# Bias rows stored with 32 repeats from the scalar engine's queue, and shifted bias tables read 32 partitions at a time

## The chip, the core and the metric

The kernel runs on one core of a Trainium2 chip. The metric is device time in microseconds (us), the median of repeated runs. The engines that matter here are the tensor engine (PE, matrix products), the vector engine (DVE), the scalar engine (ACT) and the sync engine (SP), whose queue issues nearly all transfers. All engines run beside each other, each one through its own list of instructions in order, and wait for one another by semaphores.

## What is computed

A decoder trunk for 256 tokens of width 2048: one retention layer, then one block-sparse attention layer. Each has a squared-ReLU MLP of width 8192 and a gated per-layer embedding behind it. With 256 tokens there is one attention block, so attention is plain causal attention with 16 heads of 128. What the change touches is the position bias that is added to its logits:

```python
def t5_bucket(dist):
    n = jnp.maximum(dist, 0)
    ...
    return jnp.where(n < max_exact, n, large)
...
dist_own = qpos[:, None] - (blk * BLK + jnp.arange(BLK))[None, :]
l_own = jnp.einsum('hqd,hkd->hqk', qc, k_own, ...) * scale
l_own = jnp.where(dist_own[None] >= 0, l_own + bias_t[:, t5_bucket(dist_own)], NEG_INF)
```

The bias of a head depends on the distance of query and key alone, so one row of 384 numbers for each head (distances 255 to 0, then masked places) holds everything. A table for 128 queries is this row, shifted by one place from query to query.

## The kernel before

**Weights.** The time goes into streaming some 500 MB of float32 weights through PE. Weights come in units of 128 x 1024 numbers. `load` fetches two units in one transfer of 1 MB, `raw`, on SP's queue into one of three buffers. `conv` splits a unit into a high part `wh` (a cast on ACT, L218) and a low part `wl` (a subtraction on DVE, L219), with four buffers for each. In the phases that the change touches a unit is then 8 pairs of matmuls: 512 columns with `wh` (L158) and 256 columns with `wl` (L159). `run` walks over the units. For unit i it issues the load for unit i + 6 and the conversion of unit i + 3, then the matmuls of unit i, then the small tasks that were booked for unit i with `at`. There is no scheduler: each engine gets its instructions in the order in which this loop writes them.

**Bias rows.** `bias_rows` is booked 30 units before the end of the first MLP's `mlp_dn` stream (tiles `dn`). It loads the 32 x 16 bias table and a constant 33 x 384 matrix, makes 16 rows of 384 numbers by one product (`rows`, L608, copied to `bv` by DVE, L610), and two units later writes each row many times over into the scratch tensor `bvec` in device memory (`store`, L613). The many copies are there so that `table` can read a shifted table with a plain access pattern: partition p starts at place 383 p + 127 behind the head's first number, that is at place 127 - p of copy p.

**Tables.** The attention is done in four groups of four heads. Ahead of each group `table` (L639) reads two tiles `T`, 128 partitions x 2 heads x 256 numbers. They are used some ten units later, in `logits`, where DVE adds them (L679).

**Transfers and their semaphores.** Every transfer signals one of eight semaphores, taken in turn in program order (DMAHW0 to DMAHW7 in the rows of the order below). A transfer whose predecessor on the same semaphore isn't known to have landed waits for it first. A `raw` load also waits for DVE, which must have read the buffer.

Of the kernel before, what the change touches and what calls it, by code (L numbers as in the profile page):

```python
# [10 lines left out]
F32 = mybir.dt.float32  # L11
# [6 lines left out]
P = 128  # L18
S = 256
# [5 lines left out]
AH, DH = 16, 128  # L25
GH = 4
# [7 lines left out]
LEAD = 4  # L34
LOOK = 3
WARM = 8
G_RET, G_MLP0, G_PLE0, G_KV, G_ATT, G_MLP1, G_PLE1, G_FIN = range(8)


# [34 lines left out]
class Core:  # L74
# [3 lines left out]
        self.units, self.tasks = [], {}  # L78
        self.raws, self.ready = {}, {}

# [1 line left out]
    def unit(self, src, j, mm):  # L82
        self.units.append((src, j, mm))
        return len(self.units) - 1
# [37 lines left out]
                fn()  # L122

    def steps(self, i, gen, each=1):
        """the steps of an evacuation: the first after unit i, then each of them per unit"""
        if not next(gen, True):
            self.at(i + 1, lambda: self.more(i + 1, gen, each))

# [15 lines left out]
    def small(self, name):  # L144
        return self.wp.tile([P, S], F32, name=name, tag="small", bufs=6)

# [1 line left out]
    def mm_a(self, ps, wh, wl, rhs, first, last, narrow=False):  # L148
        mm = self.nc.tensor.matmul
        for k in range(8):  # L150
# [8 lines left out]
            mm(ps[:, S:], wl[:, c], rhs[k][:, :S], start=False, stop=last and k == 7)  # L159

    def phase_a(self, name, src, base, tiles, per, lead, rhs, evac, narrow=(), rush=()):
        """tiles of [128 outputs, 256 tokens]; rhs(k) is the (H|L) tile of 128 inputs;
        a narrow tile is summed in one half of its bank"""
        banks, ends = {}, {}
        for j, (n, u) in enumerate(order_a(tiles, per, lead)):
            def mm(wh, wl, n=n, u=u):
                if u == 0:
                    banks[n] = self.bank(f"{name}{n}")
                self.mm_a(banks[n], wh, wl, [rhs(u * 8 + k) for k in range(8)], u == 0, u == per - 1, n in narrow)
            i = self.unit(src, base + j, mm)  # L170
            if u == per - 1:
                ends[n] = i
                self.at(i, lambda n=n, i=i: self.steps(i, evac(n, banks.pop(n)), 4 if n in rush else 2 if n == tiles - 1 else 1))
        return ends

    def phase_d(self, name, src, rhs, evac):
        """4 tiles of [128 outputs, 256 tokens] by units of 4 tiles of inputs and 2 of outputs"""
        banks = {}
        for u in range(4):
            for v in range(2):  # L180
                def mm(wh, wl, u=u, v=v):
                    m = self.nc.tensor.matmul
                    for n in (2 * v, 2 * v + 1):
                        if u == 0:
                            banks[n] = self.bank(f"{name}{n}")
                        ps = banks[n]
                        for j in range(4):
                            c, x = slice((4 * (n % 2) + j) * P, (4 * (n % 2) + j + 1) * P), rhs(4 * u + j)
                            m(ps, wh[:, c], x, start=u + j == 0, stop=False)
                            m(ps[:, S:], wl[:, c], x[:, :S], start=False, stop=u == 3 and j == 3)  # L190
                i = self.unit(src, 2 * u + v, mm)
                if u == 3:
                    for n in (2 * v, 2 * v + 1):
                        self.at(i, lambda n=n, i=i: self.steps(i, evac(n, banks.pop(n))))

    def phase_b(self, name, src, base, rhs, evac):
        """[256 tokens, 512 outputs] as two banks"""
        banks = []
        for u in range(KD // 2):
            def mm(wh, wl, u=u):  # L200
                if u == 0:
                    banks.extend(self.bank(f"{name}{t}") for t in range(2))
                for j in range(2):
                    k = 2 * u + j
                    x, c = rhs(k), slice(j * 512, (j + 1) * 512)
                    for t in range(2):
                        a, b = slice(t * P, (t + 1) * P), slice(S + t * P, S + (t + 1) * P)
                        mm_ = self.nc.tensor.matmul
                        mm_(banks[t], x[:, a], wh[:, c], start=k == 0, stop=False)  # L209
                        mm_(banks[t], x[:, a], wl[:, c], start=False, stop=False)  # L210
                        mm_(banks[t], x[:, b], wh[:, c], start=False, stop=k == KD - 1)  # L211
            i = self.unit(src, base + u, mm)
        self.at(i, lambda: evac(banks))
        return i

# [1 line left out]
    def split(self, dst_h, dst_l, src):  # L217
        self.nc.scalar.copy(dst_h, src)  # L218
        self.nc.vector.tensor_sub(dst_l, src, dst_h.bitcast(F32))  # L219

    def fold(self, dst, ps):
        """dst = the two halves of a bank added"""
        self.nc.scalar.copy(dst, ps[:, :S])  # L223
        self.nc.vector.tensor_add(dst, dst, ps[:, S:])  # L224

    def scaled_h(self, n, g):
        """(h * g) of tile n: the high part of H|L"""
        t = self.slot(f"x{g}_{n}", dt=F32R)
        gs = self.g[:, g, n:n + 1]
        self.nc.scalar.activation(t[:, :S], self.h[n], AF.Copy, scale=gs)  # L230
        return t
# [16 lines left out]
            self.nc.vector.tensor_add(self.acc, self.acc, sq)  # L248

    def rsqrt(self, dst, src, eps, n):  # L250
        """dst = (src + eps) ** -0.5; small tiles"""
        v = self.nc.vector
        a = self.cp.tile([P, n], F32, name="rs_a", tag="rs_a", bufs=2)
        y = self.cp.tile([P, n], F32, name="rs_y", tag="rs_y", bufs=2)
        w = self.cp.tile([P, n], F32, name="rs_w", tag="rs_w", bufs=2)
        v.tensor_scalar_add(a, src, eps)
        v.tensor_single_scalar(y.bitcast(I32), a.bitcast(I32), 1, ALU.logical_shift_right)
        v.tensor_scalar(y.bitcast(I32), y.bitcast(I32), -1, 0x5F3759DF, op0=ALU.mult, op1=ALU.add)
        for c in (3.0, 12.0, 768.0):
            v.tensor_mul(w, y, y)  # L260
            v.tensor_mul(w, w, a)
            v.scalar_tensor_tensor(y, w, c, y, op0=ALU.subtract, op1=ALU.mult)
        v.tensor_scalar_mul(dst, y, -1.0 / 8192.0)
# [22 lines left out]
        self.at(i, self.stats_a)  # L286
        self.at(i + 2, lambda: self.stats_b(**kw))

# [1 line left out]
    def start(self):  # L290
        nc, cp, io = self.nc, self.cp, self.io
        self.ones = cp.tile([P, 2], F32, name="ones")
# [2 lines left out]
        nc.scalar.activation(warm, self.ones, AF.Silu)  # L295
        self.warm(WARM)
        self.hh = [cp.tile([P, 4, S], F32, name=f"h{q}") for q in range(4)]
# [191 lines left out]
        return hi, lo  # L489

    def finish(self, n, gains):
        """tile n of the stream is whole: its scaled splits and its squares"""
        xs = [self.scaled_h(n, g) for g in gains]
        sq = self.square(n)
        yield
        for x, g in zip(xs, gains):
            self.scaled_l(n, g, x)
        self.gather(n, sq)
        self.xx[n] = xs[0]
        if len(xs) > 1:  # L500
            self.x2[n] = xs[1]
# [93 lines left out]
    def bias_rows(self, i):  # L595
        nc, cp, io = self.nc, self.cp, self.io
        st = {}

        def load():
            st["rb"] = cp.tile([33, AH], F32, name="relb")  # L600
            nc.vector.memset(st["rb"][32:33], NEG)
            nc.sync.dma_start(st["rb"][:32], io["rel_bias"])
            st["oh"] = self.slot("oh", (33, 384))
            nc.sync.dma_start(st["oh"], io["onehot"])

        def rows():
            ps = self.aux("bv")
            nc.tensor.matmul(ps[:AH, :384], st["rb"], st["oh"], start=True, stop=True)  # L608
            st["bv"] = self.slot("bv", (AH, 384))
            nc.vector.tensor_copy(st["bv"], ps[:AH, :384])  # L610

        def store():
            nc.sync.dma_start(io["bvec"], st["bv"][:, None, :].to_broadcast([AH, P, 384]))  # L613
        self.at(i, load)
        self.at(i + 6, rows)
        self.at(i + 8, store)

    def attention(self):
        nc = self.nc
        mm = nc.tensor.matmul  # L620
        first = len(self.units)
# [8 lines left out]
        for g in range(AH // GH):  # L630
            b, st = len(self.units), {}

            def table(st=st, g=g):
                st["T"] = []
                bv = self.io["bvec"]
                for j in range(0, GH, 2):
                    t = self.slot("T", (P, 2, S))
                    src = bass.AP(tensor=bv.tensor, offset=bv.offset + (g * GH + j) * P * 384 + 127, ap=[[383, P], [P * 384, 2], [1, S]])
                    nc.sync.dma_start(t, src)  # L639
                    st["T"] += [t[:, 0], t[:, 1]]  # L640
            self.at(b, table)

# [92 lines left out]
def program(nc, io):  # L735
    with tile.TileContext(nc) as tc, tc.manual_schedule(), \
# [1 line left out]
            tc.tile_pool(name="slots", bufs=59) as sp, \  # L738
            tc.tile_pool(name="psum", bufs=1, space=bass.MemoryType.PSUM) as pp, \
            tc.tile_pool(name="dram", bufs=1, space=bass.MemoryType.DRAM) as dp:  # L740
        io["bvec"] = dp.tile([AH, P, 384], F32, name="bvec")
        c = Core(nc, tc, (cp, wp, sp, pp), io)
        c.at(-1, c.start)
        c.retention()
# [71 lines left out]
```

## Time and profile before

| | |
|---|---|
| time, median of 3 runs | 2832.81 us (2832.39 to 2833.46) |
| span of the profiled execution | 2831.3 us |
| PE busy | 2798.1 us, 99% |
| DVE busy | 1807.1 us, 64% |
| ACT busy | 1347.6 us, 48% |
| moved by DMA | 521.95 MB, mean 184 GB/s |

The span runs from the first to the last instruction. The median is 1.5 us longer: that lies around the span, in starting and ending. PE is busy nearly all the time, so what counts is where PE is not, and where it is busy at less than its usual pace. The views used are the list of waits (who waited for whom), the windows (busy time and PE's granted clock in a stretch), the timeline of one engine, the chain of work that ended last, and the transfers with their time from issue to landing.

### The profile page before, as it was taken

What the parts mean: (1) busy time and instruction counts of PE and PEld (TensorE: products, weight loads), DVE (VectorE), ACT (ScalarE), POOL (GpSimd) and SP (SyncE); (2) the same over time, 40 slices, a digit from 0 to 9 for tenths busy, and PEclk for the clock granted to TensorE, in tenths of its full rate; (3) what the DMA queues carried; (4) which work ended last, traced back from release to release, by engine and by line L of the source; (5) the groups of instructions that cost most, each with busy time, mean ns of one, the idle gap of its engine ahead of it and who ended that gap; (6) DMA issues with size and microseconds to landing.
All of it is one profiled execution on the core that took longest, in us unless ns stands there. A gap on an engine that the chain in (4) does not pass through costs nothing.

```text
span 2831.3 us, 37950 instructions
## 1 busy us (share of the span) xinstructions
PE 2798.1 (99%) x15482; PEld 2417.3 (85%) x15482; DVE 1807.1 (64%) x2633; ACT 1347.6 (48%) x1901; POOL 0.2 (0%) x4
## 2 busy tenths in 40 slices
PE   9999999999999999999979999999999999999998
PEld 7888888888888888888868888888888888888887
DVE  7766666655566555665647876667665556666566
ACT  5444444444454434444436655555444434444454
POOL 0000000000000000000000000000000000000000
PEclk9999999999999999999989999999999999999998
DMA  6455555555555555555574554545555555555553
GB/s 233 179 181 181 181 182 182 182 199 186 178 194 182 190 184 189 183 189 181 191 185 179 198 181 176 180 170 185 187 184 188 183 189 186 187 190 182 194 182 119
DMA packets 78667, 521.95 MB, mean 184 GB/s; under 512 B 8443, under 2 KB 14492, under 8 KB 16796
## 3 DMA queue, kind: packets, MB, share of 16 engines
q1 hardware_dynamic: 78492, 519.52, 52.1%
q8 instruction: 121, 1.98, 0.3%
q14 instruction: 54, 0.44, 0.0%
HBM read 514.25 MB, written 5.24 MB: 183 GB/s over the span
## 4 chain that ended last, share of the span: by engine, by line
PE 98%; DMA 1%; DVE 0%; ACT 0%; SPq 0%; issue 0%; DVEq 0%; ACTq 0%
PE up L158 17%; PE dn L158 17%; PE up L159 9%; PE dn L159 8%; PE ret_out L158 4%; PE gt L158 4%; PE qk L158 4%; PE ret_out L159 2%; PE ak L158 2%; PE att_o L158 2%; PE aq L158 2%; PE v L209 2%; PE v L211 2%; PE v L210 2%; PE g L209 2%; PE g L211 2%
## 5 line engine op out<-in xcount | busy, mean ns | idle before, releaser
L219 DVE TENSOR_TENSOR wl<-raw,wh 128x1024 fp32r<-128x1024 f32 (+1 forms) x970 | 1180.9, 1221 | 643.9 <-ACT wh L218 633.0
L218 ACT CAST wh<-raw 128x1024 fp32r<-128x1024 f32 (+1 forms) x970 | 1014.6, 1049 | 774.2 <-PE dn L158 277.8
L158 PE MATMUL dn<-a,wh 128*128 128x512 f32 x2048 | 725.2, 399 | 14.5 <-ACT wh L218 14.5
L158 PE MATMUL up<-x,wh 128*128 128x512 f32 x2048 | 724.1, 399 | 0.0
L159 PE MATMUL dn<-a,wl 128*128 128x256 f32 x2048 | 576.1, 281 | 0.5 <-DVE wl L219 0.5
L159 PE MATMUL up<-x,wl 128*128 128x256 f32 x2048 | 575.1, 281 | 0.0
L158 PEld LDWEIGHTS dn<-a,wh 128*128 128x128 f32 x2048 | 385.7, 188 | 111.0 <-ACT wh L218 14.8
L158 PEld LDWEIGHTS up<-x,wh 128*128 128x128 f32 x2048 | 384.8, 188 | 95.8
L159 PEld LDWEIGHTS dn<-a,wl 128*128 128x128 f32 x2048 | 387.9, 189 | 1.0 <-DVE wl L219 1.0
L159 PEld LDWEIGHTS up<-x,wl 128*128 128x128 f32 x2048 | 387.0, 189 | 0.0
L158 PE MATMUL ret_out<-ot,wh 128*128 128x512 f32 x512 | 181.1, 399 | 0.0
L158 PE MATMUL gt<-x,wh 128*128 128x512 f32 x480 | 170.0, 399 | 0.0
L158 PE MATMUL qk<-x,wh 128*128 128x512 f32 x448 | 159.1, 399 | 0.0
L223 ACT COPY t<-up 128x256 f32<-128x256 f32 x128 | 47.6, 372 | 231.7 <-PE up L159 231.7
L159 PE MATMUL ret_out<-ot,wl 128*128 128x256 f32 x512 | 143.8, 281 | 0.0
L159 PE MATMUL gt<-x,wl 128*128 128x256 f32 x480 | 134.7, 281 | 0.0
L224 DVE TENSOR_TENSOR t<-t,up 128x256 f32<-128x256 f32 x128 | 53.9, 421 | 119.9 <-ACT t L223 119.8
L159 PE MATMUL qk<-x,wl 128*128 128x256 f32 x448 | 125.8, 281 | 0.0
L158 PEld LDWEIGHTS ret_out<-ot,wh 128*128 128x128 f32 x512 | 96.2, 188 | 24.0
L158 PEld LDWEIGHTS gt<-x,wh 128*128 128x128 f32 x480 | 90.2, 188 | 22.1
L158 PEld LDWEIGHTS qk<-x,wh 128*128 128x128 f32 x448 | 84.2, 188 | 20.3
L209 PE MATMUL v<-wh,x 128*128 128x512 f32 x256 | 100.5, 392 | 0.0
(311 smaller groups left out, 3459.3 us busy)
## 6 DMA issues: line engine op xcount, KB each, us to landing
raw<-mlp_up SPq DMA_DIRECT2D x128, 1024.0 KB, 4.9
raw<-mlp_dn SPq DMA_DIRECT2D x128, 1024.0 KB, 4.9
raw<-ret_in SPq DMA_DIRECT2D x94, 1024.0 KB, 4.9
raw<-att SPq DMA_DIRECT2D x48, 1024.0 KB, 4.9
raw<-ret_out SPq DMA_DIRECT2D x32, 1024.0 KB, 4.9
raw<-ple_gate SPq DMA_DIRECT2D x32, 1024.0 KB, 4.9
raw<-att_o SPq DMA_DIRECT2D x16, 1024.0 KB, 4.9
raw<-ple_up SPq DMA_DIRECT2D x4, 1024.0 KB, 4.9
```

Source lines behind the costliest of these rows:

```text
L158: mm(ps, wh[:, c], rhs[k], start=first and k == 0, stop=False)
L159: mm(ps[:, S:], wl[:, c], rhs[k][:, :S], start=False, stop=last and k == 7)
L209: mm_(banks[t], x[:, a], wh[:, c], start=k == 0, stop=False)
L210: mm_(banks[t], x[:, a], wl[:, c], start=False, stop=False)
L211: mm_(banks[t], x[:, b], wh[:, c], start=False, stop=k == KD - 1)
L218: self.nc.scalar.copy(dst_h, src)
L219: self.nc.vector.tensor_sub(dst_l, src, dst_h.bitcast(F32))
L223: self.nc.scalar.copy(dst, ps[:, :S])
L224: self.nc.vector.tensor_add(dst, dst, ps[:, S:])
```

## The change

`store` writes 32 copies of each row, not 128: 16 x 32 x 384 numbers (768 KB) and not 16 x 128 x 384 (3072 KB). It is issued from ACT's queue and not from SP's. `table` can then no longer read 128 partitions in one pattern, since there are only 32 copies. It reads four times 32 partitions, with a start that is q places earlier for partitions q to q + 31. What lands in `T` is the same. 8 transfers of 256 KB become 32 transfers of 64 KB, all on SP's queue. The scratch tensor shrinks accordingly. (The diff also drops some comments, which shifts no instruction.)

```diff
+BR = 32
...
         def store():
-            nc.sync.dma_start(io["bvec"], st["bv"][:, None, :].to_broadcast([AH, P, 384]))
+            nc.scalar.dma_start(io["bvec"], st["bv"][:, None, :].to_broadcast([AH, BR, 384]))
...
                 for j in range(0, GH, 2):
                     t = self.slot("T", (P, 2, S))
-                    src = bass.AP(tensor=bv.tensor, offset=bv.offset + (g * GH + j) * P * 384 + 127, ap=[[383, P], [P * 384, 2], [1, S]])
-                    nc.sync.dma_start(t, src)
+                    for q in range(0, P, BR):
+                        src = bass.AP(tensor=bv.tensor, offset=bv.offset + (g * GH + j) * BR * 384 + 127 - q, ap=[[383, BR], [BR * 384, 2], [1, S]])
+                        nc.sync.dma_start(t[q:q + BR], src)
...
-        io["bvec"] = dp.tile([AH, P, 384], F32, name="bvec")
+        io["bvec"] = dp.tile([AH, BR, 384], F32, name="bvec")
```

The order of the instructions on PE, DVE and POOL stays the same. On SP, before, the store stands between two weight loads of the `mlp_dn` stream:

```order
L96 DMA raw_11992<-mlp_dn 128x2048 [waits DMAHW7_49,DVE_49]
L96 DMA raw_12045<-mlp_dn 128x2048 [waits DMAHW2_49,DVE_49]
L613 DMA bvec<-bv 2048x1x384 [waits DVE_49]
L96 DMA raw_12093<-mlp_dn 128x2048 [waits DMAHW3_49,DVE_49]
L96 DMA raw_12142<-mlp_dn 128x2048 [waits DMAHW4_49,DMAHW0_49,DVE_49]
```

After the change it is gone from there, and stands on ACT, between two casts of weight units (`raw_11945` and `raw_11992` are consecutive loads, two casts each; the lines of the changed file are one to two higher):

```order
L219 CAST wh_12023<-raw_11945 128x1024 [waits DMAHW3_49,PE_49,Activation_49]
L219 CAST wh_12047<-raw_11945 128x1024 [waits PE_49,Activation_49]
L614 DMA bvec<-bv 512x1x384 [waits DVE_49]
L219 CAST wh_12068<-raw_11992 128x1024 [waits DMAHW4_49,PE_49,Activation_49]
L224 COPY u<-dn_10_11998 128x256 [waits PE_49]
```

The store now comes behind a cast that itself waits for PE, and the following casts come behind the store.

At the first of the four attention groups, SP before has two table reads between weight loads:

```order
L96 DMA raw_13613<-att 128x2048 [waits DMAHW0_49,DVE_49]
L96 DMA raw_13686<-att 128x2048 [waits DMAHW1_49,DVE_49]
L639 DMA T<-bvec 128x2x256 [waits PE_49] x2
L96 DMA raw_13755<-att 128x2048 [waits DMAHW2_49,DVE_49]
L96 DMA raw_13819<-att 128x2048 [waits DMAHW3_49,DVE_49]
```

and after the change it has eight:

```order
L97 DMA raw_13686<-att 128x2048 [waits DMAHW1_49,DVE_49]
L641 DMA T<-bvec 32x2x256 [waits PE_49]
L641 DMA T<-bvec 32x2x256 x3
L641 DMA T<-bvec 32x2x256 [waits PE_49]
L641 DMA T<-bvec 32x2x256 [waits DMAHW2_49]
L641 DMA T<-bvec 32x2x256 [waits DMAHW3_49]
L641 DMA T<-bvec 32x2x256 [waits DMAHW4_49]
L97 DMA raw_13761<-att 128x2048 [waits DMAHW5_49,DVE_49]
L97 DMA raw_13825<-att 128x2048 [waits DMAHW6_49,DVE_49]
```

The last three of the eight wait for the three weight loads just ahead of them (semaphores 2, 3, 4), and the next weight load waits for the first table read (semaphore 5). The other three groups look the same but for the numbers of the semaphores.

## Rows read from the trace of the kernel before

**Rows 1.** Page, part 4: chain that ended last, shares of the span.

```profile
PE 98%; DMA 1%; DVE 0%; ACT 0%; SPq 0%; issue 0%; DVEq 0%; ACTq 0%
```

**Rows 2.** Waits of PE: waiter, waited for, us in total, times, longest us.

```profile
PE dn L158 <- ACT wh L218: 14.5, 1, 14.5
PE st L269 <- DVE acc L248: 2.8, 1, 2.8
PE rb L276 <- DVE rn L263: 2.6, 1, 2.6
...
PE dn L159 <- DVE wl L219: 0.5, 1, 0.5
```

**Rows 3.** Windows: stretch, us, busy per engine, PEclk, DMA share, GB/s.

```profile
1420.00:1442.00 22.00, 22.00 (x126) 19.08 (x125) 8.04 (x10) 6.01 (x8) 0.00 (x0) 1.00 0.89 109
1442.00:1457.00 15.00, 0.51 (x3) 0.20 (x1) 0.22 (x1) 1.29 (x3) 0.00 (x0) 0.60 0.93 228
1457.00:1462.00 5.00, 4.54 (x13) 3.52 (x14) 4.25 (x6) 3.66 (x6) 0.00 (x0) 0.51 0.44 144
1462.00:1500.00 38.00, 38.00 (x225) 33.68 (x224) 25.17 (x35) 18.72 (x25) 0.00 (x0) 1.00 0.63 226
```

**Rows 4.** Chain that ended last, 1420 to 1463: start us, us, what.

```profile
1422.00 33.61 DMA raw<-mlp_dn
1455.70 1.05 ACT wh L218
1456.78 1.24 DVE wl L219
1458.06 0.58 PE dn L159
```

**Rows 5.** Page, part 6, transfers: count, KB each, median us to landing.

```profile
raw<-mlp_dn SPq DMA_DIRECT2D x128, 1024.0 KB, 4.9
...
bvec<-bv SPq DMA_DIRECT2D x1, 3072.0 KB, 35.0
T<-bvec SPq DMA_DIRECT2D x8, 256.0 KB, 5.5
```

**Rows 6.** Timeline of SP at the store: start us, us, instruction.

```profile
1416.05 0.33 SPq L96 DMA_DIRECT2D raw<-mlp_dn  x1
1417.29 0.68 SPq L613 DMA_DIRECT2D bvec<-bv  x1
```

**Rows 7.** Timeline of SP, the next load.

```profile
1422.00 6.54 SPq L96 DMA_DIRECT2D raw<-mlp_dn  x1
```

**Rows 8.** Timeline of PE at the stall; in brackets idle us before, and what ended it.

```profile
1441.79 0.40 PE L158 MATMUL dn<-a,wh 128*128 128x512 f32 x1
1442.03 0.28 PE L159 MATMUL dn<-a,wl 128*128 128x256 f32 x1
1456.80 0.80 PE L158 MATMUL dn<-a,wh 128*128 128x512 f32 x1 [14.49 <-ACT wh L218]
1458.06 0.58 PE L159 MATMUL dn<-a,wl 128*128 128x256 f32 x1 [0.46 <-DVE wl L219]
...
1462.48 0.39 PE L158 MATMUL dn<-a,wh 128*128 128x512 f32 x1
...
1498.19 0.39 PE L158 MATMUL dn<-a,wh 128*128 128x512 f32 x1
```

**Rows 9.** L158 matmuls of `dn`, ns min/median/max, first and last start; 1425 to 1441.

```profile
L158 PE MATMUL dn<-a,wh x46: 395/398/404, 1424.8 to 1440.7; 128*128 128x512 f32 x46
```

**Rows 10.** The same view, 1463 to 1498.

```profile
L158 PE MATMUL dn<-a,wh x102: 391/391/392, 1462.8 to 1497.8; 128*128 128x512 f32 x102
```

**Rows 11.** Timeline of ACT at the store and at the stall.

```profile
1419.66 1.05 ACT L218 CAST wh<-raw 128x1024 fp32r<-128x1024 f32 x1 [2.73 <-PE dn L158]
1422.49 1.05 ACT L218 CAST wh<-raw 128x1024 fp32r<-128x1024 f32 x1 [1.77 <-PE dn L158]
...
1430.98 1.05 ACT L218 CAST wh<-raw 128x1024 fp32r<-128x1024 f32 x1 [1.79 <-PE dn L158]
1455.70 1.04 ACT L218 CAST wh<-raw 128x1024 fp32r<-128x1024 f32 x1 [23.68 <-DMA raw<-mlp_dn]
```

**Rows 12.** Timeline of DVE: the copy that the store waits for.

```profile
1416.71 0.55 DVE L610 COPY bv<-bv 16x384 f32<-16x384 f32 x1 [0.68 <-PE bv L608]
```

**Rows 13.** Timeline of SP at the first attention group.

```profile
1600.21 0.33 SPq L96 DMA_DIRECT2D raw<-att  x1
1600.59 0.94 SPq L639 DMA_DIRECT2D T<-bvec  x2
1605.10 0.35 SPq L96 DMA_DIRECT2D raw<-att  x1
```

**Rows 14.** Tile `raw`, 1600 to 1606: time from issue to landing.

```profile
DMA to landing us min/median/max: 5.0/5.3/5.5
```

**Rows 15.** Timeline of ACT: the cast that uses the load issued at 1605.10.

```profile
1616.40 1.05 ACT L218 CAST wh<-raw 128x1024 fp32r<-128x1024 f32 x1
```

**Rows 16.** Tile `T`, whole span: forms, counts, ns, first and last start.

```profile
L679 DVE SCALAR_TENSOR_TENSOR lg<-lg,qs,T x32: 340/410/478, 1637.1 to 1878.4; 128x128 f32<-128x128 f32 x16, 128x256 f32<-128x256 f32 x16
L639 SPq DMA_DIRECT2D T<-bvec x8: 426/444/462, 1600.6 to 1819.0; - x8
```

**Rows 17.** Tile `out`: ten stores of 128 or 256 KB at the end.

```profile
DMA to landing us min/median/max: 1.8/2.3/2.6
```

## The prediction

> **What bounds the kernel now.** I read the chain of work that ended last first. PE has 98% of it and DMA 1% [rows 1], so the kernel is PE's own work plus a few holes. The list of PE's waits shows which holes: one of 14.5 us and one of 0.5 us in the `dn` products, both for converted weights, and two of under 3 us for statistics, which the change does not touch [rows 2]. [...] The chain says what the hole waits for: a weight load that was issued at 1422.00 and took 33.61 us, then its cast, then its subtraction, then PE [rows 4]. Such a load takes 4.9 us as a rule [rows 5]. The reason stands just ahead of it on SP's queue: the store of the bias rows, issued at 1417.29, which took 35.0 us to land [rows 5, 6], at 1452.3. The load landed at 1455.6, 3.3 us behind it. During the store the transfers move 109 GB/s at a share of 0.89; after it 226 GB/s [rows 3]. So this hole is a 1 MB load that stood in line behind a slow 3 MB store.
>
> **What the hole costs.** Before it, PE starts a pair of matmuls every (1440.7 - 1424.8) / 45 = 0.3533 us [rows 9]. From the pair at 1441.79 to the one at 1462.48 there are nine steps (seven starts lie in the rows left out) [rows 8]. Nine steps at the usual pace take 3.18 us; they took 20.69. The loss is **17.51 us**: 14.49 + 0.46 of waiting, and 2.56 of working at the lower clock.
>
> A little comes back afterwards. From 1462.48 to 1498.19 PE makes 103 steps in 35.71 us, 0.3467 us each, and its matmuls last 391 ns where they lasted 398 [rows 8 to 10]. The granted clock is 1.00 both times, so the clock is not the difference; I don't know what is. If the stream is not interrupted I take it to keep 0.3533, and lose 103 x 0.0066 = **0.68 us** of what the hole gave back. Taking the hole away is then worth 17.51 - 0.68 = **16.83 us**.
>
> **Part 1, fewer copies.** The store goes from 3072 to 768 KB. By its own rate that is 35.0 / 4 = 8.8 us to landing. The 35.0 us may hold a part that doesn't shrink; the nearest row for it is the longest landing of the small stores at the end, 2.6 us [rows 17], so the bounds are 8.8 and 11.4 us. I take 8.8, because the row is of the same transfer.
>
> How late may the weight load be before PE notices? ACT's last cast before the hole started at 1430.98. Casts of this stretch follow each other every 2.83 us (1419.66, 1422.49), each released by PE [rows 11], so the next was due at 1433.81. PE had converted weights until its next pair was due, at 1441.79 + 0.35 = 1442.14, and that pair's low part 0.24 later, at 1442.38 (1442.03 is 0.24 behind 1441.79) [rows 8]. From cast to that matmul it takes 1458.06 - 1455.70 = 2.36 us [rows 4]. So a cast at 1440.0 is early enough: PE carries **6.2 us** of late casts, and the load, which would land at 1422.00 + 4.9 = 1426.9, may land **13.1 us** late. (The trace bears this out: the load landed 15.6 us after 1440.0, and PE waited 14.95.) After the change the worst order is that the load still waits for the whole store: issued at about 1421, landing at 1432.1 by the longer bound, the load 3.3 us behind at 1435.4. That is 4.6 us earlier than 1440.0. PE does not wait, and the whole 16.83 us are gained.
>
> **Part 2, ACT's queue.** On ACT the store stands behind the cast that ended at 1420.71 and ahead of the one at 1422.49, with 1.77 us of idle time between them [rows 11]. What it waits for, the copy of `bv`, ended at 1417.26 [rows 12], so the wait costs nothing. SP needed 0.68 us to issue four times as many rows [rows 6]. In 1.77 us this is hidden. The trace shows no transfer issued by ACT, so I bound it. The longest issue of this stretch is the load's on SP just behind the store, 6.54 us [rows 7]. If ACT were held as long, to 1427.25, the cast behind would start 4.8 us late, which PE's 6.2 us still cover. If it were held for the whole store at its longer bound, to 1432.1, the cast would be 9.6 us late and PE would wait 3.4 us. I take zero; the nearest row is the store's own issue. It can't come out as a gain, since nothing of ACT's is taken away.
>
> Does the queue matter by itself? The load on SP no longer stands behind the store in one queue, so the two may share the engines and the load may land earlier still. The time is the same either way, because 1435.4 was early enough. [...] No row of this trace shows two queues at work.
>
> **Part 3, smaller table reads.** At each of four groups SP issues eight reads for two. At the first, two took 0.94 us from 1600.59 [rows 13]; a read takes at most 0.46 us to issue [rows 16], so eight take 3.7 us and end at 1604.3. The last of them waits for the load of 1600.21, which lands within 5.0 to 5.5 us, at about 1605.5 [rows 13, 14], and is issued by 1606.0. The next weight load waits also for the first read, which lands by the usual 5.5 us at 1606.1 [rows 5]. So this load goes out at 1606.1 instead of 1605.10, 1.0 us late. Nobody notices. It landed at 1610.6, and its first cast comes at 1616.40 [rows 14, 15]: 5.8 us to spare, and the 6.2 us of PE behind that, 12.0 in all. The tables are first used at 1637.1 [rows 16], 25 us after they land even so. The bytes are the same, 512 KB for a group. The cost is **zero** four times, with bounds of 0 (no reason for a gain: no wait of PE lies there [rows 2]) and, if the reads run one after another, the price of the second rival.
>
> **Sum.** 2831.3 - 16.8 = 2814.5 us of span, and with the 1.5 us around it **2816.0 us** for the median of 2832.81, -0.6%.
>
> **Rivals.** (1) *The store doesn't get shorter*: what limits it is not its bytes, and it still takes 35 us, now from about 1421. It lands at 1456, the load behind it at 1459, 3.4 us later than now, and the time is 2836.2. The point from which it decides is a landing of the load after 1440.0, so a store of over 16 us. Against it: the store is a repetition of the same 16 rows, and its rate in the windows is steady. For it: nothing shows this rate at another size. (2) *The table reads run in series and hold up the weights*; this ends on the slower side. A small transfer alone takes 2.3 us to land [rows 17]. If each read waited for the one before, eight would take 18.4 us from 1605.2 to 1623.6, and the weight load 4.9 us more, to 1628.5. It may be 12.0 us late, at 1622.6, so PE would wait 5.9 us, and with the lower clock, 2.6 us as at the hole, lose 8.5 us at each group, 34 us in all: 2850. It decides from reads that take 12 us longer than now. Against it: the two reads of now are issued within 0.94 us and land 5.5 us after issue by the median, behind a load that takes about as long [rows 5, 13, 14], so they overlap. [...] (3) *ACT is held* by the issue, as bounded above: PE waits up to 3.4 us, and with a dip of the clock 2817 to 2822. (4) *PE's faster pace comes up in more places*: 0.0066 us a pair, for a thousand pairs 6.6 us, 2809. For it: I can't say what brings it about. Against it: before the hole the slower pace is the steady one, and the order on PE doesn't change.
>
> **How the numbers follow.** A measurement of this kernel can tell about 0.2% (5.7 us) from no change. The forecast has 0.84, rival 1 0.03, rival 2 0.04, rival 3 0.05, rival 4 0.04. Faster: forecast, rivals 3 and 4, 0.93. Same: rival 1, 0.03. Slower: rival 2, 0.04. The range goes from 2812.5 (half a thousand faster pairs) to 2820 (ACT held, PE waiting for most of the 3.4 us), and holds the forecast and most of rival 3.
>
> **What the new profile would show.** Right: no wait of PE for a cast in `dn`; granted clock 1.00 from 1420 to 1500; the store on ACT with under 12 us to landing, its issue under 1 us; the loads behind it at under 14 us to landing; SP issuing eight reads in about 5 us at each group, and no wait of PE from 1600 to 1880. The pace behind 1442 tells whether the 0.68 us are lost. Wrong: a wait of PE for a cast at the store (rivals 1, 3) or in attention (rival 2), or many `dn` and `up` matmuls at 391 ns (rival 4).

## The result, and the profile after

The changed kernel takes 2815.11 us (2814.76 to 2815.45), the kernel before beside it 2833.11 us: a ratio of 0.9939 (95% interval 0.9925 to 0.9953). The forecast was 2816.0, with a range of 2812.5 to 2820.0. The profiled execution has a span of 2813.0 us.

The hole is gone. These are all waits of PE in the kernel after (waiter, waited for, us in total, times, longest us); neither line for `dn` of [rows 2] is left:

```profile
PE st L270 <- DVE acc L249: 2.8, 1, 2.8
PE rb L277 <- DVE rn L264: 2.6, 1, 2.6
PE qk L190 <- ACT wh L219: 2.3, 1, 2.3
PE warm L345 <- DVE zero L342: 1.5, 1, 1.5
```

The windows that answer to [rows 3] (stretch, us, busy per engine, PEclk, DMA share, GB/s): PE is busy throughout, the granted clock stays at 1.00 where it averaged 0.60 and 0.51 in the second and third, and the transfers move 217 GB/s where they moved 109.

```profile
1420.00:1442.00 22.00, 22.00 (x127) 19.05 (x126) 13.27 (x18) 10.36 (x14) 0.00 (x0) 1.00 0.80 217
1442.00:1457.00 15.00, 15.00 (x87) 13.04 (x86) 8.65 (x11) 6.56 (x9) 0.00 (x0) 1.00 0.55 192
1457.00:1462.00 5.00, 5.00 (x30) 4.35 (x30) 3.02 (x5) 3.19 (x5) 0.00 (x0) 1.00 0.37 154
```

The transfers of the kernel after that answer to [rows 5] (count, KB each, median us to landing):

```profile
T<-bvec SPq DMA_DIRECT2D x32, 64.0 KB, 4.3
bvec<-bv ACTq DMA_DIRECT2D x1, 768.0 KB, 9.9
```

ACT's timeline after, at the store and where the weight load behind it was needed (start us, us, instruction, idle time before it and what ended it), to be held against [rows 11]:

```profile
1418.56 1.05 ACT L219 CAST wh<-raw 128x1024 fp32r<-128x1024 f32 x1 [2.73 <-PE dn L159]
1418.86 0.66 ACTq L614 DMA_DIRECT2D bvec<-bv  x1
1421.38 1.05 ACT L219 CAST wh<-raw 128x1024 fp32r<-128x1024 f32 x1 [1.77 <-PE dn L159]
...
1432.93 1.05 ACT L219 CAST wh<-raw 128x1024 fp32r<-128x1024 f32 x1 [2.01 <-DMA raw<-mlp_dn]
```

The store took 0.66 us to issue and cost ACT nothing: the cast behind it still waited 1.77 us for PE, as before. The load behind the store was late even so. It was issued at 1420.9 and landed after 11.9 us, at 1432.8, instead of 4.9. The cast waited 2.01 us for it, but PE did not wait, because it had converted weights left.

**Where the 18 us came from.** The same two places of PE's timeline in both kernels frame the hole: the product of the bias rows, and the first product of the embedding behind the `dn` stream. First before, then after:

```profile
1415.86 0.82 PE L608 MATMUL bv<-oh,relb 33*16 33x384 f32 x2
...
1498.54 0.28 PE L563 MATMUL pu<-ph,wh 128*128 128x256 f32 x1
```

```profile
1414.75 0.81 PE L609 MATMUL bv<-oh,relb 33*16 33x384 f32 x2
...
1480.61 0.28 PE L564 MATMUL pu<-ph,wh 128*128 128x256 f32 x1
```

82.68 us became 65.86: **16.82 us**, where the sum said 16.83. The spans differ by 18.3. Of the rest, 1.11 us were there before the hole (1415.86 to 1414.75). They arise in the first 34 us, which the change doesn't touch: the first `v` product starts at 33.5 before and at 32.5 after. In the two profiled executions PE's granted clock averaged 0.83 and 0.90 in the first 12 us (before, after). The kernel before was back at 1.00 later: from 14 to 16 us it has 0.83, the kernel after 1.00. The first 12 us, before and after:

```profile
0.00:12.00 12.00, 7.89 (x21) 5.69 (x22) 3.77 (x9) 5.57 (x10) 0.20 (x4) 0.83 0.76 243
```

```profile
0.00:12.00 12.00, 8.15 (x21) 5.70 (x22) 4.88 (x10) 6.42 (x13) 0.20 (x4) 0.90 0.78 261
```

The kernel before was also timed beside later experiments, with medians of 2832.26 to 2833.56 us, so of the 18.0 us some 0.5 to 1 is such a difference between executions. 0.4 us of the spans' difference lies at the very end and was not followed up.

### The profile page after: what moved, and what is told of

Read it like the earlier page. It is cut to its first block, busy times and chain, and to the rows that moved or that the text cites. A ratio compares the mean times of both kernels' runs of the same rounds, so it can differ in the third digit from the quotient of the medians.

```text
span 2813.0 us, 37970 instructions
## 1 busy us (share of the span) xinstructions
PE 2795.0 (99%) x15482; PEld 2414.7 (86%) x15482; DVE 1807.4 (64%) x2633; ACT 1347.9 (48%) x1901; POOL 0.2 (0%) x4
## 4 chain that ended last, share of the span: by engine, by line
PE 99%; DVE 0%; DMA 0%; SPq 0%; ACT 0%; issue 0%; DVEq 0%
PE up L159 17%; PE dn L159 17%; PE dn L160 9%; PE up L160 9%; PE ret_out L159 4%; PE gt L159 4%; PE qk L159 4%; PE ret_out L160 2%; PE ak L159 2%; PE att_o L159 2%; PE aq L159 2%; PE v L210 2%; PE v L212 2%; PE v L211 2%; PE g L210 2%; PE g L212 2%
## 5 line engine op out<-in xcount | busy, mean ns | idle before, releaser
L159 PEld LDWEIGHTS qk<-x,wh 128*128 128x128 f32 x448 | 84.2, 188 | 20.3
```

The source lines that it names most:

```text
L159: mm(ps, wh[:, c], rhs[k], start=first and k == 0, stop=False)
```

## The experiments

### Which half of the change earns the gain?

**Few copies, SP's queue.** The changed kernel, with the store put back on SP's queue:

```diff
-            nc.scalar.dma_start(io["bvec"], st["bv"][:, None, :].to_broadcast([AH, BR, 384]))
+            nc.sync.dma_start(io["bvec"], st["bv"][:, None, :].to_broadcast([AH, BR, 384]))
```

> The changed kernel, but with the store of 32 copies on SP's queue. Theory (the gain is all in the fewer bytes; the load behind the store waits for it on either queue): store lands about 10 us after issue, the load behind it about 12 us after issue or less, no wait of PE in dn, 2815.1 within 1 us. Rival (the queue of ACT earns part of it): the load lands later than 13.1 us behind its usual time, PE waits again in dn, 2817 or more.

Measured: 2815.17 us, ratio 0.9938 (0.9923 to 0.9953), no wait of PE in `dn`. The store lands 10.9 us after issue, the load behind it also after 10.9, 1 us sooner than with ACT's queue. The whole gain is there without ACT. The store's line in the list of transfers:

```profile
bvec<-bv SPq DMA_DIRECT2D x1, 768.0 KB, 10.9
```

**Many copies, ACT's queue.** The kernel before, with only the queue changed:

```diff
-            nc.sync.dma_start(io["bvec"], st["bv"][:, None, :].to_broadcast([AH, P, 384]))
+            nc.scalar.dma_start(io["bvec"], st["bv"][:, None, :].to_broadcast([AH, P, 384]))
```

> The kernel before, but with the store of 128 copies on ACT's queue; the tables are read by 128 partitions each, as before. Theory (a load on the other queue still waits for the whole store): store 35 us to landing, load behind it 34 to 37 us, PE waits 14 to 18 us, 2833 to 2837. Rival (two queues share the DMA engines, so the load lands within 13 us of its usual time): no wait of PE in dn, 2815.

Measured: 2817.58 us, ratio 0.9947 (0.9933 to 0.9962). My theory fell: the load did not wait for the whole store. The store still needs 36.6 us to land (issued at 1418.5, so at 1455.1), but the load, issued at 1420.5, lands 19.1 us later, at 1439.6, and 15 us ahead of the store. The rival was not right either, since the load was 14 us late, not under 13. PE waited 1.8 us in three pieces (first the store's line, then PE's waits):

```profile
bvec<-bv ACTq DMA_DIRECT2D x1, 3072.0 KB, 36.6
```

```profile
PE dn L159 <- DVE wl L219: 1.5, 2, 0.8
PE dn L158 <- ACT wh L218: 0.3, 1, 0.3
```

PE's timeline tells the pieces apart. Only the first, 0.76 us at 1442, belongs to this load, which came at the edge of the margin. The other two (0.30 and 0.76 us, at 1459 and 1460) come from a later load, issued at 1444.5, that took 13.4 us because it met the second part of the store. Its cast waited 6.54 us for it:

```profile
1442.12 0.39 PE L159 MATMUL dn<-a,wl 128*128 128x256 f32 x1 [0.76 <-DVE wl L219]
...
1460.38 0.39 PE L159 MATMUL dn<-a,wl 128*128 128x256 f32 x1 [0.76 <-DVE wl L219]
```

```profile
1458.02 2.00 ACT L218 CAST wh<-raw 128x1024 fp32r<-128x1024 f32 x2 [6.54 <-DMA raw<-mlp_dn]
```

The windows of this run show how the two queues share (columns as above). For 14 us the store goes alone, at 99 GB/s; then both go, at 383 GB/s; then the rest of the store goes nearly alone, although another load has been issued at 1444.5:

```profile
1420.00:1434.00 14.00, 14.00 (x81) 12.12 (x81) 7.32 (x10) 5.30 (x7) 0.00 (x0) 1.00 0.89 99
1434.00:1444.00 10.00, 9.21 (x52) 7.51 (x51) 3.09 (x5) 2.91 (x5) 0.00 (x0) 1.00 1.00 383
1444.00:1453.00 9.00, 9.00 (x54) 7.93 (x53) 7.00 (x10) 5.15 (x8) 0.00 (x0) 1.00 0.90 111
```

So each half of the change does the job almost alone: the copies 17 to 18 us, the queue 15, and together no more than the copies.

### How much of the store is enough?

The changed kernel with `BR = 64` (1536 KB, ACT's queue, tables read by 64 partitions):

```diff
-BR = 32
+BR = 64
```

> The changed kernel with 64 copies (1536 KB) on ACT's queue, tables read by 64 partitions each. It measures the margin. Theory (store time goes with the bytes, 8.1 us for 512 rows so 16.2 for 1024, and the load lands 4 us behind the store; PE waits for what is later than about 1439 in this timeline): store lands about 18 us after issue, the load at about 1441, PE waits about 2 us in dn, 2817 to 2820 (the lower end if the granted clock stays up). Rival (margin larger, or the store's time not by its bytes): 2815 without a wait, or over 2825.

Measured: 2816.21 us, ratio 0.9942 (0.9925 to 0.9958). The store lands after 20.7 us (expected 18). The load, issued at 1421.1, lands after 20.3, at 1441.4 (expected about 1441), and PE waits 2.0 us, as expected (the store's line, then PE's waits in `dn`):

```profile
bvec<-bv ACTq DMA_DIRECT2D x1, 1536.0 KB, 20.7
```

```profile
PE dn L159 <- ACT wh L219: 1.2, 1, 1.2
PE dn L160 <- DVE wl L220: 0.8, 1, 0.8
```

This confirms the margin within half a microsecond: this execution ran 0.86 us ahead of the one before at the product of the bias rows (1415.00 against 1415.86), so the limit of 1440.0 lies at 1439.1 here, and the load came 2.3 us behind it. The time is 1.1 us above that of 32 copies and under the 2817 to 2820 that were expected. The granted clock stayed at 1.00, and PE ran at its other pace behind the wait (below), which gives some 0.7 us back. Between the two places that frame the hole it takes 67.64 us, 1.78 more than with 32 copies; the rest of the difference lies outside.

### Do the smaller reads cost anything?

**The reads alone.** The kernel before, with each table tile read by four transfers:

```diff
-                    nc.sync.dma_start(t, src)
+                    for q in range(0, P, 32):
+                        src = bass.AP(tensor=bv.tensor, offset=bv.offset + (g * GH + j) * P * 384 + 127 + 383 * q, ap=[[383, 32], [P * 384, 2], [1, S]])
+                        nc.sync.dma_start(t[q:q + 32], src)
```

> The kernel before, but each table tile is read by four transfers of 32 partitions; the store is as before. Theory (the smaller reads cost nothing): 2833.1 within 1 us, no wait of PE between 1600 and 1900, weight loads behind the reads 0.5 to 1 us later than before. Rival (reads in series): PE waits at the four groups, 2840 to 2867.

Measured: 2832.77 us, ratio 1.0 (0.9991 to 1.001). PE's waits are those of [rows 2], 14.6 us in `dn` among them, and none lies at the groups. SP at the first group (start us, us, instruction):

```profile
1600.32 0.33 SPq L96 DMA_DIRECT2D raw<-att  x1
1600.70 5.08 SPq L640 DMA_DIRECT2D T<-bvec  x8
1605.91 0.35 SPq L96 DMA_DIRECT2D raw<-att  x1
```

Against [rows 13], the load behind the reads goes out 0.8 us later, 0.1 of which it brought along.

**Four times as many.** The changed kernel, with reads of 8 partitions, 32 a group:

```diff
-                    for q in range(0, P, BR):
-                        src = bass.AP(..., offset=bv.offset + (g * GH + j) * BR * 384 + 127 - q, ap=[[383, BR], [BR * 384, 2], [1, S]])
-                        nc.sync.dma_start(t[q:q + BR], src)
+                    for q in range(0, P, 8):
+                        src = bass.AP(..., offset=bv.offset + (g * GH + j) * BR * 384 + 127 - q // BR * BR + 383 * (q % BR) - 0, ap=[[383, 8], [BR * 384, 2], [1, S]])
+                        nc.sync.dma_start(t[q:q + 8], src)
```

> The changed kernel, but each table tile is read by sixteen transfers of 8 partitions: 32 reads a group. It loads the margin of 12.0 us. Theory (the reads cost SP their issue, 0.43 us each, 14 us a group, and a load behind them may be 12 us late): the load behind the reads goes out 9 to 12 us late, PE waits 0 to 2 us a group, 2815 to 2823. Rival (reads in series, each paying its landing of 2 us or more): 64 us a group, PE waits over 40 us a group, over 2950.

Measured: 2816.21 us, ratio 0.9942 (0.9925 to 0.9958), 1.1 us more than with 8 reads. SP, and the cast that uses the load behind the reads:

```profile
1584.11 0.33 SPq L97 DMA_DIRECT2D raw<-att  x1
1584.49 14.70 SPq L641 DMA_DIRECT2D T<-bvec  x32
1599.29 1.86 SPq L97 DMA_DIRECT2D raw<-att  x3
```

```profile
1604.34 1.05 ACT L219 CAST wh<-raw 128x1024 fp32r<-128x1024 f32 x1 [3.94 <-DMA raw<-att]
```

32 reads take 14.70 us, 0.46 us each, and not the 64 us of a series. In the changed kernel the first read and the load behind the eight reads are at 1582.68 and 1588.02, 5.3 us apart; here they are 14.8 apart. So the load is 9.5 us later. The cast waits 3.94 us for it, and no product of the weight stream waits; PE's only waits from 1590 to 1850 are 0.6 and 0.3 us in the logits. So 9.5 us are within the margin of 12.0 us that the prediction worked out; its edge was not reached. The two waits in the logits are not in the changed kernel, and behind the hole this run takes 1.5 us more than it (1333.9 against 1332.4 us from the first product of the embedding to the end). So 32 reads a group are not quite free; that the late casts cause these waits was not followed up.

### Why is the store slow?

The 16 rows of `bv` lie on 16 partitions, and all 2048 rows of the store are read from there. Here the kernel before makes the rows eight times over, on 128 partitions, and stores each of them 16 times. Queue, bytes and row length stay.

```diff
+        def widen():
+            st["rw"] = cp.tile([33, P], F32, name="relw")
+            nc.vector.tensor_copy(st["rw"].rearrange("p (h r) -> p h r", r=8), st["rb"][:, :, None].to_broadcast([33, AH, 8]))
...
-            nc.tensor.matmul(ps[:AH, :384], st["rb"], st["oh"], start=True, stop=True)
-            st["bv"] = self.slot("bv", (AH, 384))
-            nc.vector.tensor_copy(st["bv"], ps[:AH, :384])
+            nc.tensor.matmul(ps[:, :384], st["rw"], st["oh"], start=True, stop=True)
+            st["bv"] = self.slot("bv", (P, 384))
+            nc.vector.tensor_copy(st["bv"], ps[:, :384])
...
-            nc.sync.dma_start(io["bvec"], st["bv"][:, None, :].to_broadcast([AH, P, 384]))
+            nc.sync.dma_start(io["bvec"].rearrange("h (r k) c -> (h r) k c", r=8), st["bv"][:, None, :].to_broadcast([P, 16, 384]))
...
+        self.at(i + 5, widen)
```

> The kernel before (SP's queue, 128 copies, 3072 KB, tables read by 128 partitions), but the 16 rows are made eight times over, on 128 partitions (a small DVE copy widens the bias table first), and each partition is stored 16 times. Theory (the store is slow because all its rows are read from 16 partitions): 3 MB from 128 partitions go at the rate of the weight loads, about 3.3 us a MB, store 10 to 13 us to landing, no wait of PE in dn, 2815 to 2816. Rival (writing 2048 rows of 1536 bytes to device memory is slow in itself): 35 us, PE waits 14 to 15 us, 2833.

Measured: 2814.48 us, ratio 0.9937 (0.9922 to 0.9952). The line of the store, to be held against the 35.0 us of [rows 5]:

```profile
bvec<-bv SPq DMA_DIRECT2D x1, 3072.0 KB, 14.0
```

The same 3072 KB from 128 partitions land in 14.0 us, 219 KB a us against 88. So the store was slow because of where it reads, not because of the number and size of the rows that it writes. Each partition is also read fewer times here, 16 and not 128, but that doesn't set the rate: from 16 partitions, the store goes at 98 GB/s with 32 copies (1422 to 1426), at 96 with 64 and at 99 with 128 (1420 to 1434) while it has the engines alone, in the three runs with ACT's queue. Why 16 partitions give no more than that, no run here shows.

This third way, with every copy kept and the reads unsplit, is as fast as the change. The last 0.6 us are not the store's: behind the wider product of the bias rows the `dn` stream runs at the quicker pace (below), and the two places that frame the hole lie 64.74 us apart, 1.1 less than after the change:

```profile
L158 PE MATMUL dn<-a,wh x36: 391/391/391, 1417.8 to 1429.9; 128*128 128x512 f32 x36
```

### What does a load on the other queue wait for?

The kernel of the last experiment, with its store on ACT's queue:

```diff
-            nc.sync.dma_start(io["bvec"].rearrange(...), ...)
+            nc.scalar.dma_start(io["bvec"].rearrange(...), ...)
```

> The kernel with the rows made on 128 partitions (2048 rows stored, tables read by 128 partitions), its store on ACT's queue. It asks what a load on the other queue waits for: with 512, 1024 and 2048 rows stored from 16 partitions it landed 11.9, 20.3 and 19.1 us after issue. Theory (it waits for about the first 1024 rows, whatever their pace, and then shares): half of a store that takes some 9 us, so the load lands 8 to 10 us after issue. Rival A (it waits for a stretch of time, some 14 us): it lands later than 14 us. Rival B (it waits for the whole store when that is short): 11 to 13 us. The time is 2814 to 2816 in each case.

Measured: 2814.59 us, ratio 0.9933 (0.991 to 0.9955). The store, issued at 1419.9, lands after 17.1 us, at 1437.0; the load, issued at 1422.0, lands after 10.1 us, at 1432.1, 5 us ahead of the store. That is just above the 8 to 10 us of the theory, whose store of some 9 us was put too short.

```profile
bvec<-bv ACTq DMA_DIRECT2D x1, 3072.0 KB, 17.1
```

So it waits neither for a fixed stretch of time (rival A) nor for the whole store (rival B). The list of transfers splits the bytes by queue (packets, MB, share of 16 engines; q10 is ACT's queue, a packet is a row here, and q1 is SP's). From 1421 to 1426 it has this one line, although the load was issued at 1422.0:

```profile
q10 hardware_dynamic: 1080, 1.66, 98.0%
```

From 1426 to 1432 q1 moves 1.14 MB and q10 1.08. So a head piece of the store goes first, and then the two share. In the 2048-row store from 16 partitions that piece took 14 us at 99 GB/s, 1.39 MB or some 900 rows of 1536 bytes; with 64 copies it is some 905 of 1024 rows (96 GB/s, 1420 to 1434.5). With 512 and 1024 rows in all, the load landed behind the store. So the piece is counted in rows rather than in time: some 900 to 1100 rows, in 14 us or in 5. That is as if some 1000 rows were already lined up ahead of the load when it came; that this is the mechanism was not shown.

### What sets PE's pace at the full clock?

The prediction left open why PE makes a pair in 0.3467 us behind the hole and in 0.3533 ahead of it. The experiment with 64 copies gave a hint. Behind its short wait, with the clock at 1.00 throughout, PE went on at 391 ns a matmul (columns as in [rows 9]):

```profile
L159 PE MATMUL dn<-a,wh x105: 391/391/392, 1445.9 to 1481.9; 128*128 128x512 f32 x105
```

In the run with many copies on ACT's queue a wait switched it on, and the next wait switched it off again:

```profile
L158 PE MATMUL dn<-a,wh x42: 391/391/391, 1443.7 to 1458.0; 128*128 128x512 f32 x42
```

```profile
L158 PE MATMUL dn<-a,wh x47: 395/398/403, 1461.7 to 1477.9; 128*128 128x512 f32 x47
```

So it is not the clock, and not the waiting as such. The probe puts small products, which nothing reads, between the units of the second layer's `up` stream, eight in each half of it:

```diff
+        first = len(self.units)
+        def extra(n):
+            ps = self.aux("ex")
+            x = self.xx[0]
+            nc.tensor.matmul(ps[:, :n], x[:, :P], x[:, :n], start=True, stop=True)
+        for half in range(2 if layer else 0):
+            for j in range(8):
+                self.at(first + (0 if half == 0 else 128) + 6 + 7 * j, lambda n=(64 if half == 0 else 32) + 64 * j: extra(n))
```

> The changed kernel with 16 extra small products, never read, every seventh unit of the second layer's up stream: 64 to 512 columns in steps of 64 in its first half, 32 to 480 in its second half. It asks what sets PE's pace of 398 or 391 ns for the 512-column products at the full granted clock. Theory (the pace is set by how PE comes back into the alternating stream, so an extra product of some length flips it): some of the 16 stretches run at 391 ns. Rival (only a wait of PE flips it): all 16 at 398. Time 2815 plus up to 4 us for the products, less up to 0.4 us for each stretch that is flipped.

Measured: 2805.56 us in one run, 9.6 below the changed kernel, more than expected, because the pace also held in the streams behind. The stretch behind the first product (64 columns) and the one behind the second (128 columns):

```profile
L159 PE MATMUL up<-x,wh x52: 395/398/403, 1991.9 to 2009.9; 128*128 128x512 f32 x52
```

```profile
L159 PE MATMUL up<-x,wh x53: 391/391/391, 2010.7 to 2028.8; 128*128 128x512 f32 x53
```

The product of 128 columns switched the pace on. PE still had it behind six more products of 192 to 512 columns, and in the `dn` units between the two halves (from 2128):

```profile
L159 PE MATMUL dn<-a,wh 128*128 128x512 f32 x512 | 177.5, 391 | 0.0
```

In the second half of `up`, PE was at 398 ns again behind the products of 160 and 352 columns, and at the quicker pace behind those of 288 and 416 (then 392 to 395 ns, with the same 0.3467 us a pair). Which length does what I can't say. A guess, not shown, is that it depends on where in the stream's rhythm PE comes back. What brings the two rhythms about stays open.

The last run uses this. The changed kernel gets thirteen extra products, twelve at the starts of the long streams and one in `dn`, behind the product of the bias rows:

```diff
+    def extra(self, i, n):
+        def one():
+            ps = self.aux("ex")
+            self.nc.tensor.matmul(ps[:, :n], self.now[:, :P], self.now[:, :n], start=True, stop=True)
+        self.at(i, one)
...
             self.units[i][2](wh, wl)
+            self.now = wh
...
+        self.extra(len(self.units) + 8, 128)
+        self.extra(len(self.units) + 14, 256)
         self.phase_a(src, src, 0, KD, per, LEAD, rhs, evac)
...
         self.stats(len(self.units) + 4, squared=True)
+        self.extra(len(self.units) + 10, 128)
+        self.extra(len(self.units) + 18, 256)
+        if layer == 0:
+            self.extra(len(self.units) + 256 - 30 + 11, 128)
...
         self.stats(b + 4)
+        self.extra(b + 12, 128)
+        self.extra(b + 18, 256)
```

> The changed kernel with thirteen extra products, never read, of 128 or 256 columns: two behind the start of each long stream (ret_out, up of both layers, gt of both layers, att_o), one behind the bias rows' product in dn. The runs before showed that such a product can switch the steady pace of a stream from 0.3533 to 0.3467 us a pair and that the pace then holds until the next interruption. Theory (it does so in most streams): some 4000 to 5000 pairs at 0.0066 us less, less 13 products of 0.1 to 0.2 us: 2783 to 2795. Rival (the switch in the probe was an accident of that place): 2812 to 2818, with most streams at 398 ns.

Measured: **2785.75 us**, ratio to before 0.9834 (0.982 to 0.9847), 29.4 us below the changed kernel. Every long stream that got a product, or follows one that did, runs faster; `qk`, which got none, stays at 399. In the changed kernel all of these have 399 ns, as in its line for `up` (first; then those of this run; line, engine, operation, count | busy us, mean ns):

```profile
L159 PE MATMUL up<-x,wh 128*128 128x512 f32 x2048 | 724.1, 399 | 0.0
```

```profile
L166 PE MATMUL dn<-a,wh 128*128 128x512 f32 x2048 | 711.6, 394 | 0.0
L166 PE MATMUL up<-x,wh 128*128 128x512 f32 x2048 | 711.6, 394 | 0.0
L166 PE MATMUL ret_out<-ot,wh 128*128 128x512 f32 x512 | 178.6, 395 | 0.0
L166 PE MATMUL gt<-x,wh 128*128 128x512 f32 x480 | 168.1, 394 | 0.0
L166 PE MATMUL qk<-x,wh 128*128 128x512 f32 x448 | 159.1, 399 | 0.0
L166 PE MATMUL att_o<-o,wh 128*128 128x512 f32 x256 | 89.9, 396 | 0.0
```

## Why the prediction was right

**The hole and its price.** Right in mechanism and size: a weight load behind the slow store. 17.51 us of loss less 0.68 of quicker work afterwards made 16.83; the frame around the hole gives 16.82. The 0.68 us were lost as forecast. In the kernel after, `dn` runs at the usual pace from 1442 on, as in [rows 9] and not as in [rows 10]:

```profile
L159 PE MATMUL dn<-a,wh x109: 395/398/404, 1441.7 to 1479.9; 128*128 128x512 f32 x109
```

**Part 1, the bytes.** The store's landing was put at 8.8 us, with bounds to 11.4; it took 9.9. The load was to land by 1435.4 at the latest and landed at 1432.8. The margin (1440.0, which is 1439.1 in the timeline of that run) was confirmed by the run with 64 copies, whose load came at 1441.4 and made PE wait 2.0 us. Rival 1, a store that doesn't get shorter, is ruled out: 9.9, 20.7 and 36.6 us for 32, 64 and 128 copies.

**Part 2, ACT's queue.** Zero was right: 0.66 us of issue, hidden, and rival 3 did not come about. The store was not issued in the idle time behind the cast, as the prediction had it, but during that cast, 0.3 us after its start. A guess of that part was wrong: that the load might land earlier on a queue of its own. It landed after 11.9 us beside ACT's store and 10.9 behind SP's. So the other queue gained nothing in the changed kernel (2815.11 us with it, 2815.17 without). By itself it did: with the full 3072 KB the move was worth 15 us, because the load on SP's queue waited some 14 us for a part of the store, and not 36.6 us for all of it.

**Part 3, the reads.** Zero was right. Eight reads took 5.24 us (forecast about 5), and the load behind them was some 0.8 us late (forecast 1.0): it goes out 5.34 us after the first read, where it went 4.51 us after it in [rows 13]. SP in the kernel after:

```profile
1582.68 5.24 SPq L641 DMA_DIRECT2D T<-bvec  x8
1588.02 0.37 SPq L97 DMA_DIRECT2D raw<-att  x1
```

Rival 2 is ruled out by the reads alone (ratio 1.0) and by 32 reads a group, which took 0.46 us each.

**The sum.** 2816.0 against 2815.1. The 0.9 us are not in the change: in the profiled executions 1.1 us lie in the first 34 us and 0.4 at the very end, and the median lies 2.1 us above the profiled span, where 1.5 were put. The hole's part came out within 0.01 us; the run with the reads alone has 82.72 us between the same two places where the kernel before has 82.68, so the second decimal is luck.

**Rival 4** did not come about in the changed kernel, but the pace it speaks of is worth more than the change.

## What to carry to other kernels

When the engine that bounds a kernel stands still once, look for the transfer that stood ahead of the late one on the same queue: fewer bytes or a source spread over more partitions each removed this hole alone, and another queue left 1.8 us of it. Work out by how much a load may be late before the bounding engine notices (here 13 us), and compare each cost off the path with that; it told beforehand that the three parts of the change cost nothing. Look also at the pace of the steady stretches: two rows of the same matmul at 391 and 398 ns at the same granted clock were worth more here than the hole.

## What was not expected of the hardware

- The steady streams of alternating 512- and 256-column matmuls showed two paces at a granted clock of 1.00, 0.3533 and 0.3467 us a pair. A single extra product (of 128 columns, in the probe) or a short wait (of 2.0 us, with 64 copies) switched between them, and the quicker pace was still there in 512 pairs of `dn` at 391 ns. Thirteen extra products were worth 29.4 us.
- A load on SP's queue waited some 14 us for a long store on ACT's queue, and then overtook it by 15 us. What it waited for was some 900 to 1100 rows of the store, whether they took 14 us (from 16 partitions) or 5 us (from 128).
- A store of the same 3072 KB landed in 35.0 us from 16 partitions and in 14.0 us from 128.
- ACT issued its store 0.3 us after the start of a cast of 1.05 us that stands ahead of it, so this issue did not wait for the instruction ahead of it to end.
